# Negated rounding on ScalarE and an adding transfer for four weight tiles of the last feed-forward, with the rearrangement moved from the scaled inputs to their high and low parts

## Chip, cores and metric

The kernel runs on one core of one Trainium2 chip. The metric is the time of one execution in device microseconds, the median of several runs; less is better. Before the change it was 848.21 us (three runs, 847.84 to 849.12).

## The reference, cut to what matters

One decoder layer on 512 tokens of 1024 channels, all in float32: a half-step SwiGLU feed-forward, a mixer (a gated recurrence beside sliding-window attention), and a second half-step feed-forward, each between two RMS norms. The change touches the weights and the inputs of the feed-forwards.

```python
def swiglu(x, w_gu, w_down):
    gate, up = jnp.split(x @ w_gu, 2, axis=-1)
    return (jax.nn.silu(gate) * up) @ w_down

x = x + 0.5 * rms_norm(swiglu(rms_norm(x, ffn1_pre_g[l]), ffn1_w_gu[l], ffn1_w_down[l]), ffn1_post_g[l])
...
x = x + 0.5 * rms_norm(swiglu(rms_norm(x, ffn2_pre_g[l]), ffn2_w_gu[l], ffn2_w_down[l]), ffn2_post_g[l])
```

`w_gu` has 2 x 2816 columns, `w_down` is 2816 x 1024.

## The kernel before, in words

**Products in three passes.** Every matrix operand is held as a high part, which is the value rounded to the matrix engine's float32r format, and a low part, which is the value minus the high part. A product is high x high, high x low and low x high, summed in PSUM. So each weight tile needs a rounding copy (ScalarE, `act.copy`, line 208) and a subtraction (`low.tensor_sub`, line 213, by default on VectorE) before TensorE can use it. TensorE runs 4580 matmuls in all.

**The weight stream.** The class `Weights` holds one list of units in the order of their use. A raw block is loaded from HBM by SyncE (line 173) into one of five buffers with the tag `raw`; a unit is one weight tile made from it: `cast` is the rounding copy, `low` the subtraction. `take` hands the next unit to TensorE and first calls `fill`, which issues the casts and lows of the units that lie 3 or 4 further on. When the last unit of a raw block has had its low part issued, the next raw block's load is issued; it goes to the buffer that has been free the longest, and so waits until the readers of that buffer's last block are done. SyncE is one queue in order: a load that waits holds up every load and store behind it. While the residual stream `xT` occupies two of the five raw buffers (up to the end of the stage below), three are left.

**The stage of the change.** In the last feed-forward the first six blocks of 128 hidden channels are done in the plain way (`Hidden.classic`): for f = 2 to 5 a product `pgb` for the gate and a product `pub` for the up half, each 24 matmuls of 512 columns. Then `classic_down` multiplies by the first six blocks of rows of `ffn2_w_down`. Its weights are the units `bd`: `add_down` makes raw block `bd00` (rows f = 0 to 3, left half of the columns) with the tiles `bd00` and `bd20`, raw block `bd40` with tile `bd40`, then `bd01` with `bd01` and `bd21`, and `bd41` (right half). A tile is 128 x 1024 numbers and feeds 24 matmuls (lines 1826, 1827 and 1828: hidden high x weight high, hidden high x weight low, hidden low x weight high). Right behind it `octo(6)` begins, a Strassen-like scheme of seven products on combined weights, whose raw blocks are `bx60`, `bx61`, `by60` and `by61` and whose first weight tiles are `bp` from `bx60` and from `bx61`.

**Beside it**, spread over the same products, VectorE prepares the combined inputs of those seven products. `Next.sums(k)` scales two channel blocks by their gain and the norm factor (`xa`, `xb`, line 635), forms four differences (lines 639 to 642), and ScalarE rounds them (lines 638 and 644); `Next.lows(k)` makes their low parts (lines 651 and 655). This is done for k = 0 to 3 in each feed-forward. The tokens of these inputs stand in a rearranged order, in pieces of 32 tokens, which the scaling writes: four `scalar_tensor_tensor` per block, each for a quarter. VectorE also transposes the residual stream (`z`, line 1836), which SyncE writes to HBM as `x_hbm` in four transfers for each block (line 1839).

**Other users of the queues.** GpSimd multiplies the up and gate halves (`usb`, line 809) and issues transfers: the plain stores of partial outputs (line 1866) and, elsewhere in the program, transfers that add a tile of 128 x 512 numbers to what stands in HBM (line 1095, `accum_op=ALU.add`).

The order on each engine is the order of the code; nothing is reordered.

Of the kernel before, what the change touches and what calls it, by code (L numbers as in the profile page):

```python
# [121 lines left out]
def tile_layer(ctx: ExitStack, tc: tile.TileContext, out: bass.AP, **ins: bass.AP):  # L122
    nc = tc.nc
    pe, dve, act, pool, sync = nc.tensor, nc.vector, nc.scalar, nc.gpsimd, nc.sync
# [12 lines left out]
    HALF = [slice(0, T // 2), slice(T // 2, T)]  # L137
# [39 lines left out]
    class Deferred:  # L177


        def tensor_sub(self, *args):  # L180
            self.args = args
# [13 lines left out]
    deferred, shared = Deferred(), Shared()  # L195

    def w_tiles(nk, c, name):
        return (wpool.tile([P, nk, c], F32R, tag="whi", name=f"whi_{name}", bufs=NWS),
# [2 lines left out]
    def add_unit(r, part, nk, c, name, low=dve):  # L201
        def two(t, like):
            return t.rearrange("p k (i d) -> p k i d", i=2) if len(like.shape) == 4 else t

        def cast(raw):
            x, (hi, lo) = part(raw), w_tiles(nk, c, name)
            for ks in shared.parts if low is shared else [slice(0, nk)]:
                act.copy(two(hi, x)[:, ks], x[:, ks])
            return hi, lo

        def take_low(raw, hi, lo):
            x = part(raw)
            low.tensor_sub(two(lo, x), x, two(hi.bitcast(F32), x))

        W.unit(r, cast, take_low)
# [169 lines left out]
    def add_down(f, n, dh):  # L385

        r = W.raw(lambda: load_raw([ins["ffn2_w_down"][0, f * P:(f + n) * P, dh * T:(dh + 1) * T]], n, T, f"bd{f}{dh}"))
        for i in range(0, n, 2):
            add_unit(r, lambda raw, i=i: raw[:, i:i + 2, :], 2, T, f"bd{f + i}{dh}")

    for g, (f0, f1) in enumerate(GROUPS2):
        if g == 0:
# [174 lines left out]
    x_tiles, xT = stream()  # L567
# [8 lines left out]
    def x_low(x, src, gain, sl):  # L576
        dve.scalar_tensor_tensor(x[1][:, sl], src, gain, x[0].bitcast(F32)[:, sl], op0=ALU.mult, op1=ALU.subtract)

    def dealt(t):

        return t.rearrange("p (i b n) -> p b i n", b=NB, n=32)

    class Next:


        def __init__(self, name, pre=None, gain=None, dealt=False):

            self.name, self.pre, self.dealt = name, pre, dealt
# [32 lines left out]
        def sums(self, k):  # L621


            n = f"{self.name}{k}"
            xa, xb, t13, t24 = (wt(f"{s}_{n}") for s in ("xa", "xb", "ta", "tb"))
            b11 = t2k(f"b11_{n}", F32R)
            highs = [t2k(f"{s}h_{n}", F32R) for s in ("b2", "t13", "t24")]
            l, r = HALF
            for x, c in ((xa, k), (xb, k + 4)):
                if self.dealt:  # L630
                    d = x.rearrange("p (b i n) -> p b i n", b=NB, n=32)
                    for i in range(4):
                        row = slice(i * P, (i + 1) * P)
                        xi, ri = (t[:, row].rearrange("p (b n) -> p b n", b=NB) for t in (xT[c], self.R))
                        dve.scalar_tensor_tensor(d[:, :, i], xi, self.gain(c), ri, op0=ALU.mult, op1=ALU.mult)
                else:
                    dve.scalar_tensor_tensor(x, xT[c], self.gain(c), self.R, op0=ALU.mult, op1=ALU.mult)
            act.copy(b11[:, l], xa[:, l])
            dve.tensor_sub(t13[:, l], xa[:, r], xa[:, l])
            dve.tensor_sub(t13[:, r], xb[:, r], xa[:, r])  # L640
            dve.tensor_sub(t24[:, l], xb[:, r], t13[:, l])
            dve.tensor_sub(t24[:, r], xb[:, l], t24[:, l])
            for h, x in zip(highs, (xb, t13, t24)):
                act.copy(h, x)
            self.made = n, xa, b11, highs, (xb, t13, t24)

        def lows(self, k):

            n, xa, b11, highs, xs = self.made
            l, r = HALF  # L650
            dve.tensor_sub(b11[:, r], xa[:, l], b11.bitcast(F32)[:, l])
# [141 lines left out]
    class Hidden:  # L793
# [68 lines left out]
        def quad(self, f, last, ahead, beside=lambda i: None):  # L862

            n = f"{self.name}{f}"
            l, r = HALF
            hs = [(t2k(f"hh{n}{j}", F32R), t2k(f"hl{n}{j}", F32R)) for j in range(2)]

            def seven(b, form, first, ahead=AHEAD):
                hi, lo = W.take(ahead)
                for j in range(2):  # L870
                    o, js = b[:, HALF[j]], slice(j * P, (j + 1) * P)
                    for k in range(4):
                        xh, xl = self.nxt.t[form, k]
                        for i, (w, x) in enumerate(((hi, xh), (hi, xl), (lo, xh))):
                            pe.matmul(o, w[:, k, js], x, start=first and i + j + k == 0, stop=k == 3 and i == 2, skip_group_check=True)  # L875

            def low_parts(x, h):
                def own(t):
                    return dealt(t)[:, 2 * h:2 * h + 2] if self.nxt.dealt else t[:, HALF[h]]

                def like(t):
                    return t.rearrange("p (b i n) -> p b i n", b=2, n=32) if self.nxt.dealt else t

                for j in range(2):
                    act.copy(own(hs[j][0]), like(x[:, HALF[j]]))
                for j in range(2):
                    hh, hl = hs[j]
                    dve.tensor_sub(own(hl), like(x[:, HALF[j]]), own(hh.bitcast(F32)))
# [24 lines left out]
            dve.tensor_add(u2, u2, D)  # L913
            dve.tensor_mul(u2, p1, u2)
            W.later(1, low_parts, u2, 0)
            beside(5)
            seven(A, "b22", False, ahead)
            act.activation(g1, A, AF.Silu)
            beside(6)
            if last:  # L920
                last_half()
                low_parts(g1, 1)
            else:
                W.later(1, last_half)
                W.later(2, low_parts, g1, 1)
            for j in range(2):
                self.hs[f + j] = hs[j]
# [170 lines left out]
        return {(0, 0): B, (1, 0): Dd, (0, 1): E_, (1, 1): A}  # L1098


    n1 = Next("a", gain=lambda c: g1[:, c:c + 1], dealt=True)
    ssx = const.tile([P, 2 * NB], F32, name="ssx")
    g1 = const.tile([P, KD], F32, name="g1")

# [236 lines left out]
    for g, (f0, f1) in enumerate(GROUPS1):  # L1341
# [18 lines left out]
        for c in range(KD):  # L1360
# [25 lines left out]
            b = pair_banks[c] if c < 2 else product(W.take(), xs, name=f"ya{g}{c}")  # L1386
# [93 lines left out]
    for j in range(4):  # L1480
        b = in_product(f"pq{j}")
# [83 lines left out]
    hl = us_  # L1565
# [5 lines left out]
    scale = HD ** -0.5  # L1571
# [242 lines left out]
            W.fill(3)  # L1814
    late = [(c, W.take(0)) for c in range(EARLY, KD)]

    n2 = Next("f2", "ffn2_pre_g", dealt=True)
    banks = boundary(res, late, ysp, None, n2, "m")


# [75 lines left out]
    for g, (f0, f1) in enumerate(GROUPS2):  # L1896
# [9 lines left out]
        hs = hid.classic(f1, banks, {2.5: turns[:2], 3: turns[2:4], 3.5: [(n2.sums, 0)], 4: [(n2.lows, 0)] + turns[4:6], 4.5: [(n2.sums, 1)], 5: [(n2.lows, 1)] + turns[6:]}, AHEAD - 1)  # L1906
# [96 lines left out]
```

## Time and profile before

| | us |
|---|---|
| median of three runs | 848.21 (847.84 to 849.12) |
| the profiled execution's own time | 847.59 |
| its span, first to last instruction | 845.8 |
| TensorE busy with matmuls | 837.5 |
| VectorE busy | 726.3 |
| ScalarE busy | 516.2 |
| GpSimd busy | 187.8 |

The profile shows one execution. The span is what its rows cover; the 1.8 us between span and own time lie around it. A matmul's row is 389 ns long for 512 columns, but matmuls overlap, and the rate is read from the distance of their starts. In the list of instructions in order of time a row holds the start, the time taken, the engine, the line, the operation, what it writes and reads, and in brackets the idle time before it with what ended it. Names are those of the tiles, with buffer numbers left out, so that `wlo_bd` stands for the low part of each of the six `bd` tiles; in the rows on normalised inputs `_f` stands for the last feed-forward.

### The profile page before, as it was taken

The numbers are of one execution on the slowest core, as the hardware profiler recorded it, in microseconds if no ns is written. First come the engines' busy times: TensorE is split into PE (matmuls) and PEld (weight loads), VectorE is DVE, ScalarE is ACT, GpSimd is POOL, SyncE is SP. The second block draws the span as 40 slices with busy tenths as digits, with TensorE's granted clock in tenths as the row PEclk, the third lists the DMA queues.
The fourth block names the chain that finished last, engine by engine and source line by source line (L and its number), as shares of the span: only waits on it lengthen the run. The fifth ranks groups of instructions, "written<-read, shape, count | busy, mean of one in ns | idle before, by whom it ended". The sixth has DMA issues, their size and how long they took to land.

```text
span 845.8 us, 12561 instructions
## 1 busy us (share of the span) xinstructions
PE 837.5 (99%) x4580; PEld 727.3 (86%) x4580; DVE 726.3 (86%) x1054; ACT 516.2 (61%) x855; POOL 187.8 (22%) x199
## 2 busy tenths in 40 slices
PE   9999999999999999999999999999999999999996
PEld 8988888988988998998788899888888888888885
DVE  4988999988979866889989589698969999898996
ACT  6646856676666655556788447335655667666562
POOL 2023000230320334434455045110200014032001
PEclk9999999999999999999999999999999999999999
DMA  7249429397594899231311130166740939769742
GB/s 251 76 135 333 157 68 325 76 246 253 141 255 166 179 273 326 69 101 50 102 49 51 50 124 28 56 141 192 259 150 18 309 95 247 252 150 256 302 138 100
DMA packets 120990, 138.50 MB, mean 164 GB/s; under 512 B 23440, under 2 KB 81120, under 8 KB 120416
## 3 DMA queue, kind: packets, MB, share of 16 engines
q1 hardware_dynamic: 108816, 110.81, 40.9%
q0 software_dynamic: 11968, 26.75, 14.4%
q8 instruction: 36, 0.59, 0.3%
q14 instruction: 26, 0.21, 0.1%
q10 hardware_dynamic: 144, 0.13, 0.0%
HBM read 100.45 MB, written 37.22 MB: 163 GB/s over the span
## 4 chain that ended last, share of the span: by engine, by line
PE 97%; DVE 1%; POOL 1%; ACT 0%; issue 0%; DVEq 0%; POOLq 0%; ACTq 0%
PE aa L948 10%; PE ab L948 10%; PE db L948 5%; PE da L948 5%; PE yaa L1326 3%; PE bb L948 3%; PE ba L948 3%; PE yda L1326 2%; PE ya L501 2%; PE ya L500 2%; PE ya L499 2%; PE a_first L1185 1%; PE aa L875 1%; PE yb L1828 1%; PE yb L1827 1%; PE yb L1826 1%
## 5 line engine op out<-in xcount | busy, mean ns | idle before, releaser
L1095 POOL DMA_DIRECT2D yp_a<-stage x42 | 36.8, 1072 | 180.8 <-ACT stage L1092 162.8
L1095 POOL DMA_DIRECT2D yp_b<-stage x28 | 24.2, 1024 | 138.1 <-ACT stage L1092 122.8
L499 PE MATMUL ya<-hha,whi_ad 128*128 128x512 f32 x62 | 24.1, 389 | 0.0
L500 PE MATMUL ya<-hla,whi_ad 128*128 128x512 f32 x62 | 24.1, 389 | 0.0
L501 PE MATMUL ya<-hha,wlo_ad 128*128 128x512 f32 x62 | 24.1, 389 | 0.0
L682 POOL TENSOR_TENSOR acca_r<-acca_r,sq_r 128x512 f32<-128x512 f32 x6 | 8.0, 1327 | 45.4 <-ACT sq_r L530 45.4
L1962 POOL TENSOR_TENSOR last<-yp,grow 128x512 f32<-128x512 f32 x3 | 3.9, 1291 | 58.4 <-DVE yp L1957 58.4
L518 PE MATMUL an<-xh_mx,whi_xl 128*128 128x256 f32 x64 | 15.8, 287 | 0.0
L1958 ACT ACTIVATE ysq<-yp 128x512 f32<-128x512 f32 (+1 forms) x9 | 5.3, 585 | 16.9 <-DVE yp L1957 16.6
L519 PE MATMUL an<-xh_mx,wlo_xl 128*128 128x256 f32 x64 | 15.5, 283 | 0.0
L809 POOL TENSOR_TENSOR usb<-usb,gsb 128x512 f32<-128x512 f32 x5 | 6.4, 1295 | 35.3 <-DVE usb L806 24.0
L499 PE MATMUL gt<-xh_mx,whi_gt 128*128 128x512 f32 x32 | 14.2, 444 | 0.0
L501 PEld LDWEIGHTS ya<-hha,wlo_ad 128*128 128x128 f32 x62 | 11.6, 188 | 2.4
L500 PEld LDWEIGHTS ya<-hla,whi_ad 128*128 128x128 f32 x62 | 11.6, 188 | 2.4
L499 PEld LDWEIGHTS ya<-hha,whi_ad 128*128 128x128 f32 x62 | 11.6, 188 | 2.4
L499 PE MATMUL pub<-xh_f,whi_bu 128*128 128x512 f32 x32 | 12.6, 395 | 0.0
L501 PE MATMUL gt<-xh_mx,wlo_gt 128*128 128x512 f32 x32 | 12.6, 394 | 0.0
L499 PE MATMUL pgb<-xh_f,whi_bg 128*128 128x512 f32 x32 | 12.6, 393 | 0.0
L499 PE MATMUL pq<-xh_mx,whi_q 128*128 128x512 f32 x32 | 12.6, 393 | 0.0
L500 PE MATMUL gt<-xl_mx,whi_gt 128*128 128x512 f32 x32 | 12.6, 392 | 0.0
L501 PE MATMUL pq<-xh_mx,wlo_q 128*128 128x512 f32 x32 | 12.5, 390 | 0.0
L501 PE MATMUL pgb<-xh_f,wlo_bg 128*128 128x512 f32 x32 | 12.5, 390 | 0.0
(1962 smaller groups left out, 3502.7 us busy)
## 6 DMA issues: line engine op xcount, KB each, us to landing
yp_a<-stage POOLq DMA_DIRECT2D x50, 256.0 KB, 8.9
yp_b<-stage POOLq DMA_DIRECT2D x36, 256.0 KB, 9.1
h_a<-za SPq DMA_DIRECT2D x16, 256.0 KB, 4.5
hxa<-h_a SPq DMA_DIRECT2D x16, 256.0 KB, 19.0
h_b<-zb SPq DMA_DIRECT2D x16, 256.0 KB, 4.0
hxb<-h_b SPq DMA_DIRECT2D x16, 256.0 KB, 7.3
xn<-in_x SPq DMA_DIRECT2D x8, 256.0 KB, 4.7
xT_hbm<-xT POOLq DMA_DIRECT2D x2, 1024.0 KB, 9.6
```

The source lines that it names most:

```text
L499: pe.matmul(ps, hi[:, k, :], xh, start=start, stop=False)
L500: pe.matmul(ps, hi[:, k, :], xl, start=False, stop=False)
L501: pe.matmul(ps, lo[:, k, :], xh, start=False, stop=stop)
L518: pe.matmul(ps[:, sl], hi[:, k, :], xh, start=k == 0, stop=False)
L519: pe.matmul(ps[:, sl], lo[:, k, :], xh, start=False, stop=False)
L875: pe.matmul(o, w[:, k, js], x, start=first and i + j + k == 0, stop=k == 3 and i == 2, skip_group_check=True)
L948: pe.matmul(b[tb], x[:, blk], w[:, k, :], start=first and q + k + j == 0, stop=q + k == 2 and j == 2, skip_group_check=True)
L1095: pool.dma_start(o, st.rearrange("p (a b) -> p a b", a=2) if len(o.shape) == 3 else st, accum_op=ALU.add)
L1185: pe.matmul(banks[j][:, HALF[0]], ws[j][part][:, k, :], n1.xs[k][xpart][:, HALF[0]], start=k == 0 and part == xpart, stop=stop and k == KD ...
L1326: pe.matmul(o, a[:, k, ms], x[:, js], start=first and i + k + m % 2 == 0, stop=k == 1 and i == 2, skip_group_check=True)
L1826: pe.matmul(ps, hh[:, blk], hi[:, k, cs], start=start, stop=False, **kw)
L1827: pe.matmul(ps, hh[:, blk], lo[:, k, cs], start=False, stop=False, **kw)
```

## The change

**The low part of four weight tiles.** A class `Added` stands in for VectorE in `add_unit`. For `bd00`, `bd20`, `bd01` and `bd21` (`f + i < 4`) the low part is no longer one VectorE subtraction: ScalarE writes the negated high part into the low tile, and GpSimd issues a transfer from the raw block (in SBUF) to the low tile (in SBUF) that adds, so that raw minus high stands there. `bd40` and `bd41` keep the subtraction.

**The order of the tokens.** The scaling in `Next.sums` now writes in the natural order, one instruction per block instead of four. The four differences work on views of that (`sides`), and the rearrangement is made when ScalarE rounds (it reads through `dealt` and writes in order) and when VectorE subtracts the high part (which reads `dealt`). This holds for both feed-forwards. In `low_parts` of `quad` only the names change, since both users had the rearranged order before.

The core of the diff:

```diff
+    class Added:
+        def tensor_sub(self, lo, x, hi):
+            act.activation(lo, hi, AF.Copy, scale=-1.0)
+            pool.dma_start(lo.bitcast(F32), x, accum_op=ALU.add)
...
         for i in range(0, n, 2):
-            add_unit(r, lambda raw, i=i: raw[:, i:i + 2, :], 2, T, f"bd{f + i}{dh}")
+            add_unit(r, lambda raw, i=i: raw[:, i:i + 2, :], 2, T, f"bd{f + i}{dh}", added if f + i < 4 else dve)
...
-    def dealt(t):
-        return t.rearrange("p (i b n) -> p b i n", b=NB, n=32)
+    def dealt(t, s=slice(0, 2)):
+        return t.rearrange("p (i b n) -> p b i n", b=NB, n=32)[:, 2 * s.start:2 * s.stop]
+    def in_turn(t):
+        return t.rearrange("p (b i n) -> p b i n", i=NB, n=32)
+    def sides(t):
+        t = t.rearrange("p (i s m) -> p s i m", s=2, m=64)
+        return t[:, 0], t[:, 1]
...
             for x, c in ((xa, k), (xb, k + 4)):
-                if self.dealt:
-                    d = x.rearrange("p (b i n) -> p b i n", b=NB, n=32)
-                    for i in range(4):
-                        row = slice(i * P, (i + 1) * P)
-                        xi, ri = (t[:, row].rearrange("p (b n) -> p b n", b=NB) for t in (xT[c], self.R))
-                        dve.scalar_tensor_tensor(d[:, :, i], xi, self.gain(c), ri, op0=ALU.mult, op1=ALU.mult)
-                else:
-                    dve.scalar_tensor_tensor(x, xT[c], self.gain(c), self.R, op0=ALU.mult, op1=ALU.mult)
-            act.copy(b11[:, l], xa[:, l])
-            dve.tensor_sub(t13[:, l], xa[:, r], xa[:, l])
...
+                dve.scalar_tensor_tensor(x, xT[c], self.gain(c), self.R, op0=ALU.mult, op1=ALU.mult)
+            (al, ar), (bl, br), (t1, t3), (t2, t4) = (sides(x) for x in (xa, xb, t13, t24))
+            act.copy(in_turn(b11[:, HALF[0]]), dealt(xa, slice(0, 1)))
+            dve.tensor_sub(t1, ar, al)
...
             for h, x in zip(highs, (xb, t13, t24)):
-                act.copy(h, x)
+                act.copy(in_turn(h), dealt(x))
...
-                dve.tensor_sub(lo, x, h.bitcast(F32))
+                dve.tensor_sub(in_turn(lo), dealt(x), in_turn(h.bitcast(F32)))
```

On VectorE, before, around the first two of the four tiles (`usb4` is the scaled up product of f = 4, `f21` the inputs of k = 1):

```order
L1836 STREAM_TRANSPOSE z5_6069<-xT1_3462 128x512
L213 TENSOR_TENSOR wlo_bd00_6076<-raw_bd00_5966,whi_bd00_6075 128x1024
L806 TENSOR_TENSOR usb4_6104<-pub4_6079,R_f2_5848 128x512
L635 SCALAR_TENSOR_TENSOR xa_f21_6107<-xT0_3461,cols_137,R_f2_5848 128x4x32 x4
L635 SCALAR_TENSOR_TENSOR xb_f21_6108<-xT1_3462,cols_137,R_f2_5848 128x4x32 x4
L639 TENSOR_TENSOR ta_f21_6109<-xa_f21_6107 128x256
L640 TENSOR_TENSOR ta_f21_6109<-xb_f21_6108,xa_f21_6107 128x256
L641 TENSOR_TENSOR tb_f21_6110<-xb_f21_6108,ta_f21_6109 128x256
L642 TENSOR_TENSOR tb_f21_6110<-xb_f21_6108,tb_f21_6110 128x256
L213 TENSOR_TENSOR wlo_bd20_6132<-raw_bd00_5966,whi_bd20_6131 128x1024
L815 TENSOR_TENSOR hlb4_6163<-usb4_6104,hhb4_6162 128x512
```

The same place of VectorE in the changed kernel (its lines are numbered some 7 higher):

```order
L1840 STREAM_TRANSPOSE z5_6039<-xT1_3438 128x512
L813 TENSOR_TENSOR usb4_6075<-pub4_6050,R_f2_5824 128x512
L643 SCALAR_TENSOR_TENSOR xa_f21_6078<-xT0_3437,cols_137,R_f2_5824 128x512
L643 SCALAR_TENSOR_TENSOR xb_f21_6079<-xT1_3438,cols_137,R_f2_5824 128x512
L646 TENSOR_TENSOR ta_f21_6080<-xa_f21_6078 128x4x64
L647 TENSOR_TENSOR ta_f21_6080<-xb_f21_6079,xa_f21_6078 128x4x64
L648 TENSOR_TENSOR tb_f21_6081<-xb_f21_6079,ta_f21_6080 128x4x64
L649 TENSOR_TENSOR tb_f21_6081<-xb_f21_6079,tb_f21_6081 128x4x64
L822 TENSOR_TENSOR hlb4_6129<-usb4_6075,hhb4_6128 128x512
```

Both `wlo` subtractions are gone from VectorE's row, and eight quarter scalings have become two whole ones.

On ScalarE, in the changed kernel, from the rounding of `bd00` to that of the fifth tile (`hhb4`, `hhb5` are the rounded hidden blocks, `gsb5` a Silu):

```order
L215 CAST whi_bd00_6045<-raw_bd00_5942 128x1024
L199 ACTIVATE wlo_bd00_6046<-whi_bd00_6045 128x1024
...
L651 CAST t24h_f21_6085<-tb_f21_6081 128x512
L215 CAST whi_bd20_6096<-raw_bd00_5942 128x1024
L199 ACTIVATE wlo_bd20_6097<-whi_bd20_6096 128x1024
L821 CAST hhb4_6128<-usb4_6075 128x512
...
L821 CAST hhb5_6188<-usb5_6185 128x512
L215 CAST whi_bd01_6196<-raw_bd01_6101 128x1024
L199 ACTIVATE wlo_bd01_6197<-whi_bd01_6196 128x1024
L215 CAST whi_bd21_6201<-raw_bd01_6101 128x1024
L199 ACTIVATE wlo_bd21_6202<-whi_bd21_6201 128x1024
L215 CAST whi_bd41_6209<-raw_bd41_6158 128x1024
```

Each of the four rounding copies now has a second instruction of the same size right behind it; the rest of ScalarE's order is as before.

On GpSimd, in the changed kernel, between the products of f = 3 and the first stores:

```order
L816 TENSOR_TENSOR usb3_5969<-usb3_5969,gsb3_5923 128x512
L200 DMA wlo_bd00_6046<-raw_bd00_5942 128x1024
L816 TENSOR_TENSOR usb4_6075<-usb4_6075,gsb4_6023 128x512
L200 DMA wlo_bd20_6097<-raw_bd00_5942 128x1024
L200 DMA wlo_bd01_6197<-raw_bd01_6101 128x1024
L200 DMA wlo_bd21_6202<-raw_bd01_6101 128x1024
L1870 DMA yp_b00_5759<-stage_6320 128x512
```

The four adding transfers are new there. SyncE's order is unchanged, but two of its loads now wait for these transfers: `raw_bd41`, which takes the buffer of `raw_bd00`, and `raw_bx61`, which takes the buffer of `raw_bd01`; before, they waited for VectorE's subtractions.

More of the change, by code (lines that the diff above doesn't have):

```diff
@@ L193, in tensor_sub @@
                 eng.tensor_sub(lo[:, ks], x[:, ks], hi[:, ks])
-    deferred, shared = Deferred(), Shared()
+    class Added:
+        def tensor_sub(self, lo, x, hi):
+            act.activation(lo, hi, AF.Copy, scale=-1.0)
+            pool.dma_start(lo.bitcast(F32), x, accum_op=ALU.add)
+    deferred, shared, added = Deferred(), Shared(), Added()
     def w_tiles(nk, c, name):
@@ L577, in x_low, with __init__ @@
         dve.scalar_tensor_tensor(x[1][:, sl], src, gain, x[0].bitcast(F32)[:, sl], op0=ALU.mult, op1=ALU.subtract)
-    def dealt(t):
-        return t.rearrange("p (i b n) -> p b i n", b=NB, n=32)
+    def dealt(t, s=slice(0, 2)):
[5 more added lines that the diff above has]
+        return t[:, 0], t[:, 1]
     class Next:
-        def __init__(self, name, pre=None, gain=None, dealt=False):
-            self.name, self.pre, self.dealt = name, pre, dealt
+        def __init__(self, name, pre=None, gain=None):
+            self.name, self.pre = name, pre
             self.gain = gain or (lambda c: col(pre, c))
@@ L627, in sums @@
             highs = [t2k(f"{s}h_{n}", F32R) for s in ("b2", "t13", "t24")]
-            l, r = HALF
             for x, c in ((xa, k), (xb, k + 4)):
-                if self.dealt:
-                    d = x.rearrange("p (b i n) -> p b i n", b=NB, n=32)
-                    for i in range(4):
-                        row = slice(i * P, (i + 1) * P)
-                        xi, ri = (t[:, row].rearrange("p (b n) -> p b n", b=NB) for t in (xT[c], self.R))
-                        dve.scalar_tensor_tensor(d[:, :, i], xi, self.gain(c), ri, op0=ALU.mult, op1=ALU.mult)
-                else:
-                    dve.scalar_tensor_tensor(x, xT[c], self.gain(c), self.R, op0=ALU.mult, op1=ALU.mult)
[L638 to L642, printed above, removed]
+                dve.scalar_tensor_tensor(x, xT[c], self.gain(c), self.R, op0=ALU.mult, op1=ALU.mult)
+            (al, ar), (bl, br), (t1, t3), (t2, t4) = (sides(x) for x in (xa, xb, t13, t24))
+            act.copy(in_turn(b11[:, HALF[0]]), dealt(xa, slice(0, 1)))
+            dve.tensor_sub(t1, ar, al)
+            dve.tensor_sub(t3, br, ar)
+            dve.tensor_sub(t2, br, t1)
+            dve.tensor_sub(t4, bl, t2)
             for h, x in zip(highs, (xb, t13, t24)):
-                act.copy(h, x)
+                act.copy(in_turn(h), dealt(x))
             self.made = n, xa, b11, highs, (xb, t13, t24)
@@ L650, in lows @@
             l, r = HALF
-            dve.tensor_sub(b11[:, r], xa[:, l], b11.bitcast(F32)[:, l])
+            dve.tensor_sub(in_turn(b11[:, r]), dealt(xa, slice(0, 1)), in_turn(b11.bitcast(F32)[:, l]))
             self.t["b11", k] = b11[:, l], b11[:, r]
@@ L878, in own @@
                 def own(t):
-                    return dealt(t)[:, 2 * h:2 * h + 2] if self.nxt.dealt else t[:, HALF[h]]
-                def like(t):
-                    return t.rearrange("p (b i n) -> p b i n", b=2, n=32) if self.nxt.dealt else t
+                    return dealt(t, slice(h, h + 1))
                 for j in range(2):
-                    act.copy(own(hs[j][0]), like(x[:, HALF[j]]))
+                    act.copy(own(hs[j][0]), in_turn(x[:, HALF[j]]))
                 for j in range(2):
                     hh, hl = hs[j]
-                    dve.tensor_sub(own(hl), like(x[:, HALF[j]]), own(hh.bitcast(F32)))
+                    dve.tensor_sub(own(hl), in_turn(x[:, HALF[j]]), own(hh.bitcast(F32)))
             def last_half():
@@ L1098, in seven_down @@
         return {(0, 0): B, (1, 0): Dd, (0, 1): E_, (1, 1): A}
-    n1 = Next("a", gain=lambda c: g1[:, c:c + 1], dealt=True)
+    n1 = Next("a", gain=lambda c: g1[:, c:c + 1])
     ssx = const.tile([P, 2 * NB], F32, name="ssx")
@@ L1815, in tile_layer @@
     late = [(c, W.take(0)) for c in range(EARLY, KD)]
-    n2 = Next("f2", "ffn2_pre_g", dealt=True)
+    n2 = Next("f2", "ffn2_pre_g")
     banks = boundary(res, late, ysp, None, n2, "m")
```

## The prediction

> **What bounds the kernel now.** I read the page's busy times first, then the shares of the chain that ended last, then the busy time by stretches.
>
> ```profile
> PE 837.5 (99%) x4580; PEld 727.3 (86%) x4580; DVE 726.3 (86%) x1054; ACT 516.2 (61%) x855; POOL 187.8 (22%) x199
> PE 97%; DVE 1%; POOL 1%; ACT 0%; issue 0%; DVEq 0%; POOLq 0%; ACTq 0%
> 0.00:42.00 42.00, 40.54 (x286) 38.38 (x287) 30.84 (x84) 27.65 (x56) 5.13 (x9) 1.00 0.51 165
> 42.00:85.00 43.00, 43.00 (x191) 35.63 (x190) 36.59 (x67) 23.47 (x38) 11.05 (x13) 1.00 0.68 234
> 550.00:592.00 42.00, 42.00 (x187) 34.79 (x186) 37.22 (x71) 18.65 (x27) 2.59 (x2) 1.00 0.64 166
> 592.00:634.00 42.00, 42.00 (x187) 34.79 (x186) 33.92 (x42) 26.01 (x36) 4.36 (x8) 1.00 0.59 207
> ```
>
> TensorE (PE) is 97% of the chain. The last four rows give a stretch, its length, the busy time of PE, PE's weight loads, VectorE, ScalarE and GpSimd, the granted clock, and the DMA share and rate. The two upper ones hold the inputs' sums for the first feed-forward, the lower two the stage of the four tiles and the start of the octo. From 42 us on PE is busy for the whole length in each of them, at full clock. A busy PE could still be a slow one, so I look at the chain in order of time for the spacing:
>
> ```profile
> 575.29 0.23 PE yb L1827
> 580.73 0.23 PE yb L1827
> 591.61 0.23 PE yb L1827
> 607.70 5.44 PE ab L948 x24
> ```
>
> The first three rows are the first matmuls that read the low parts of `bd00`, `bd20` and `bd01`: these are the deadlines. They stand 5.44 us apart for each tile of 24 matmuls, the same 5.44 us that 24 matmuls take in the octo behind. So PE runs at its own pace here and waits for nobody. VectorE, 86% busy, is busy beside it. **The change therefore has nothing to gain at this place**, only deadlines to miss: no wait of PE ends with a VectorE instruction that it removes. In the first 42 us PE lacks 1.46 us; its waits show one row:
>
> ```profile
> PE warm L1172 <- POOL ident masks.py:199: 1.4, 1, 1.4
> ```
>
> That is the start of the program, which the change doesn't touch. Shorter sums in the first feed-forward give PE nothing either.
>
> **What the change removes from VectorE and adds to ScalarE.**
>
> ```profile
> 556.66 1.13 DVE L635 SCALAR_TENSOR_TENSOR xb_f<-xT,cols,R_f 128x128 f32<-128x128 f32 x4
> 566.59 1.18 DVE L213 TENSOR_TENSOR wlo_bd<-raw_bd,whi_bd 128x1024 fp32r<-128x1024 f32 x1
> 574.66 1.23 DVE L213 TENSOR_TENSOR wlo_bd<-raw_bd,whi_bd 128x1024 fp32r<-128x1024 f32 x1 [1.64 <-ACT whi_bd L208]
> 575.81 0.68 DVE L815 TENSOR_TENSOR hlb<-usb,hhb 128x512 fp32r<-128x512 f32 x1
> 584.51 2.36 DVE L213 TENSOR_TENSOR wlo_bd<-raw_bd,whi_bd 128x1024 fp32r<-128x1024 f32 x2 [0.26 <-ACT whi_bd L208]
> L577 DVE SCALAR_TENSOR_TENSOR yll<-xc,cols,ylh x4: 750/751/752, 472.6 to 479.2; 128x512 fp32r<-128x512 f32 x4
> L639 DVE TENSOR_TENSOR ta_f<-xa_f x4: 409/413/414, 557.7 to 601.4; 128x256 f32<-128x256 f32 x4
> L888 DVE TENSOR_TENSOR hla<-u2a,hha x2: 418/421/424, 314.5 to 314.8; 128x256 fp32r<-128x256 f32 x2
> L638 ACT CAST b_f<-xa_f x4: 396/407/407, 556.8 to 600.5; 128x256 fp32r<-128x256 f32 x4
> L885 ACT CAST hha<-u2a x2: 401/401/401, 314.0 to 314.3; 128x256 fp32r<-128x256 f32 x2
> ```
>
> Rows of neighbours overlap by some 0.08 us (the row at 574.66 ends at 575.89, the next starts at 575.81). Four subtractions go, 4 x 1.15 = 4.6 us. Four quarter scalings take 1.13 us together; one whole one takes 0.75 - 0.08 = 0.67 against 1.05, so a block saves 0.38, a `sums` 0.76, eight of them 6.1 us. The new views in pieces cost nothing that I can see: the 128x256 subtraction in pieces of 32 (line 888) takes 0.42 us, the contiguous one (line 639) 0.41; the ScalarE copies (lines 885 and 638) 0.40 and 0.41. I take zero, for both engines. VectorE loses 10.7 us of work, all of it beside PE: worth nothing by itself. It does make the engine earlier, which is needed below.
>
> ScalarE's rows give the times at which the four tiles are rounded:
>
> ```profile
> 563.95 1.04 ACT L208 CAST whi_bd<-raw_bd 128x1024 fp32r<-128x1024 f32 x1
> 573.59 1.04 ACT L208 CAST whi_bd<-raw_bd 128x1024 fp32r<-128x1024 f32 x1
> 582.91 0.62 ACT L814 CAST hhb<-usb 128x512 fp32r<-128x512 f32 x1 [4.15 <-DVE usb L809]
> 583.44 2.00 ACT L208 CAST whi_bd<-raw_bd 128x1024 fp32r<-128x1024 f32 x2
> 592.51 1.05 ACT L283 CAST whi_bp__6330<-raw_bx__6296 128x1024 fp32r<-128x1024 f32 x1 [0.46 <-DMA raw_bx__6296<-in_ffn_w_gu]
> 593.47 2.05 ACT L1865 ACTIVATE stage<-yb 128x512 f32<-128x512 f32 x4
> ```
>
> The negated copy has the size of the rounding copy, so I give it the same 1.04 us. It reads what that one wrote and so starts when it has ended. A round plus a negation is 2.1 us; four negations are 4 us of ScalarE, which is idle for 4.15 us ahead of `hhb` alone.
>
> **The new transfer** is the term that decides. The trace has no addition from SBUF to SBUF of 512 KB. Its nearest rows are the additions of 256 KB into HBM (line 1095), the first and the last two of eight on end, and the plain stores of 256 KB (line 1866), each with the time from issue to landing:
>
> ```profile
> L1095 POOL DMA_DIRECT2D yp_b<-stage x1: 852/852/852, 750.6 to 750.6; - x1
> DMA to landing us min/median/max: 6.7/6.7/6.7
> ...
> L1095 POOL DMA_DIRECT2D yp_b<-stage x2: 850/1016/1183, 757.3 to 757.8; - x2
> DMA to landing us min/median/max: 11.0/11.6/12.2
> ...
> L1866 POOL DMA_DIRECT2D yp_b<-stage x8: 539/539/606, 594.3 to 608.6; - x8
> DMA to landing us min/median/max: 2.4/4.2/6.0
> ```
>
> The first, with none ahead of it, takes 6.7 us. The eight from 750.6 land from 757.3 (750.6 + 6.7) to 770.0 (757.8 + 12.2): 12.7 us for seven distances, 1.8 us for each 256 KB. So twice the bytes should take 6.7 + 1.8 = **8.5 us**, two on end 3.6 us apart. The bounds: a plain 256 KB at its fastest, 2.4 us, twice that is 4.8; and twice the lone addition, 13.4. I take 8.5, since additions are the nearer kind.
>
> Here the Trainium skill says something else. "DMA: Bandwidth & Descriptors", section "Anatomy of one DMA", fits such a GpSimd transfer as about 2.0 us plus its bytes at 436 GB/s; 512 KB would then take 3.2 us, an estimate from that page, and every tile would be some 5 us early. The plain stores' 2.4 us agree with it (it gives 2.6), the additions' 6.7 us do not, and the sum goes by these.
>
> **The deadlines, one by one.**
>
> `bd00`: rounded at 563.95, or up to 0.76 earlier by the shorter sums; 563.2 + 2.1 gives the issue at 565.3 and the landing at 573.8. Wanted at 575.29. In time.
>
> `bd20`: ScalarE rounds it behind the sums of k = 1. They come 0.76 + 1.15 + 0.76 = 2.7 us earlier (two sums, one subtraction gone), so 573.59 becomes 570.9, the issue 573.0, the landing 581.5. Wanted at 580.73: **0.8 us late**, and PE waits.
>
> `bd01`: VectorE no longer waits 1.64 us for `bd20`, but its next instruction, `hlb`, waits for ScalarE's `hhb`, now behind the negation: about 573.6 in place of 575.81, 2.2 us earlier. `hhb` of f = 5 follows at 580.7 and `bd01` is rounded at 581.2, issued at 583.4, landed at 591.9. Wanted at 591.61, moved by 0.8: in time. `bd21` lands 3.6 us later, at 595.5; its deadline is 5.44 us after `bd01`'s, 597.05. In time.
>
> **What else waits.** GpSimd's multiply `usb4` stands behind the first transfer's issue and still comes before VectorE hands it its input. SyncE's loads matter more:
>
> ```profile
> 579.88 4.16 SPq L1839 DMA_DIRECT2D x_hbm<-z  x8
> 584.14 0.46 SPq L173 DMA_DIRECT2D raw_bd<-in_ffn_w_down  x1
> 586.90 0.88 SPq L173 DMA_DIRECT2D raw_bx__6296<-in_ffn_w_gu  x2
> 595.91 1.21 DVE L287 TENSOR_TENSOR wlo_bp__6331<-raw_bx__6296,whi_bp__6330 128x1024 fp32r<-128x1024 f32 x1
> 605.15 0.42 DVE L651 TENSOR_TENSOR b_f<-xa_f,b_f 128x256 fp32r<-128x256 f32 x1
> 610.26 0.62 PE L948 MATMUL ab<-whi_bp__6330,b_f 128*128 128x512 f32 x2
> ```
>
> `raw_bd41` needs `bd20`'s transfer, 581.5, and stood behind the `x_hbm` stores until 584.14 anyway (581.9 now): no loss. `raw_bx61` needs `bd21`'s, 595.5 in place of 586.90: 8.6 us later, and `by60` queues behind it. Its rounding moves from 592.51 to 601.1, in front of four stage copies (2.05 us) and the next rounding on ScalarE. From the low part of `bp` to the last `b_f` low VectorE took 605.15 - 595.91 = 9.2 us; less 0.76, and 0.7 for a rounding behind the stage copies, that is 9.1 from 602.2, with its own 0.4: 611.7. PE reads it four matmuls after 610.26, at 611.2, moved by 0.8 to 612.0. In time by 0.3 us.
>
> **Sum:** 0.8 us of waiting once, nothing gained: 847.59 + 0.8 = 848.4 for the profiled execution, 0.6 us under the median shown, so 848.21 + 0.8 = **849.0**. All three tight deadlines turn at a landing of 7.7 to 8.2 us (580.73 - 573.0 for `bd20`, 591.61 - 583.4 for `bd01`); beyond, each further us costs one.
>
> **Rivals.** (1) *Hidden.* The destination in SBUF answers faster than HBM, the landing stays under 7.7 us, PE never waits: 848.2. For it: the plain stores' 2.4 us and the skill's formula; against: every addition of half the size took at least 6.7. Chance 0.18. (2) *Slower than before by over 0.2%*: the landing time grows with the bytes as a whole, or the loads of `bd41` and `bx60` (1.5 MB beside `bd01`'s transfer) stretch it. At 13.4 us `bd20` lands at 586.4, 5.7 us late, and the octo's path moves as much: 853.9. It counts as slower from a landing of 9.4 us, 1.7 us late, at 849.9. For it: the additions that were queued took 11 to 12.2 us; against: those had seven ahead of them. Chance 0.36. (3) *Faster*: an earlier VectorE shortens what the chain spends on VectorE, 1% of the span or some 8 us; a fifth of it would give 846.5. Against: the chain runs on PE wherever the sums and the four tiles stand. Chance 0.04. (4) That the adding transfer doesn't free VectorE because `hlb` waits for ScalarE instead is in the sum already (2.2 in place of 2.7 us).
>
> **How the numbers follow.** Forecast 0.42, the rivals 0.18, 0.36, 0.04. A measurement of this kernel can tell about 0.2%, 1.7 us, from no change: within it are the forecast and the hidden case, 0.60; slower 0.36, faster 0.04. The range goes from a hidden transfer with 0.5 us of scatter, 847.7, to a landing near 12.5 us, 853.0; it leaves out the end of rival 2 and rival 3, under 2 in 10.
>
> **What would show it.** The landing of the four adding transfers: 8.5 us, 3.6 apart for the last two. PE's first read of `bd20`'s low part at 581.5 behind a wait for that DMA. `raw_bx61` issued near 595.5, released by a transfer. The scalings as single rows of 0.75 us. Wrong would be: a landing under 7 us, a wait of PE at `bd00`, differences in pieces that take more than 0.45 us, or a time below 847.

## The result, and the profile after

| | before | after |
|---|---|---|
| median, us | 847.87 (847.12 to 849.12, 15 runs) | 849.15 (848.01 to 850.43, 15 runs) |
| the profiled execution's own time, us | 847.59 | 849.90 |
| its span, us | 845.8 | 848.2 |

The changed kernel takes 1.0014 times as long (95% interval 1.0008 to 1.0021), 1.28 us more: within 0.2%, as forecast, and still a loss that can be told from nothing. The profiled execution lies 0.75 us above its median; its matmuls already reach the stage of the change 0.84 us later than before's did (the first read of `bd00`'s low part, below, is at 575.97, and at 575.13 in before). A second profile of the same kernel, further down, doesn't show this shift, so I compare places by their distances.

The page of after, busy times, the chain's shares and the costliest group with a wait:

```profile
PE 838.4 (99%) x4580; PEld 727.4 (86%) x4580; DVE 715.8 (84%) x1002; ACT 519.0 (61%) x859; POOL 193.4 (23%) x203
PE 89%; DVE 3%; DMA 2%; ACT 2%; issue 2%; POOL 1%; SPq 1%; DVEq 0%; POOLq 0%; ACTq 0%
L1831 PE MATMUL yb<-wlo_bd,hs 128*128 128x512 f32 x32 | 12.6, 395 | 1.0 <-DMA wlo_bd<-raw_bd 1.0
```

VectorE (DVE) is down from 726.3 to 715.8 us, as the change intends, and it bought nothing. A DMA is now in the chain, and the matmuls on a low part of the `bd` tiles have waited 1.0 us for one. The two longest of TensorE's waits over the whole of after (engine, line, released by: total, times, longest; the two others listed are of 0.2 us each, and neither stands in this stage):

```profile
PE warm L1176 <- POOL ident masks.py:199: 1.4, 1, 1.4
PE yb L1831 <- DMA wlo_bd<-raw_bd: 1.0, 1, 1.0
```

The first row was there before. The second is new, and it happened once. Which of the four tiles was it? TensorE's rows in order of time at the first reads of `bd00`, `bd20` and `bd01`:

```profile
575.97 0.39 PE L1831 MATMUL yb<-wlo_bd,hs 128*128 128x512 f32 x1
...
581.18 0.39 PE L1830 MATMUL yb<-whi_bd,hs 128*128 128x512 f32 x1
581.41 0.44 PE L1831 MATMUL yb<-wlo_bd,hs 128*128 128x512 f32 x1
...
592.12 0.39 PE L1830 MATMUL yb<-whi_bd,hs 128*128 128x512 f32 x1
593.55 0.50 PE L1831 MATMUL yb<-wlo_bd,hs 128*128 128x512 f32 x1 [1.04 <-DMA wlo_bd<-raw_bd]
593.89 0.40 PE L1832 MATMUL yb<-whi_bd,hs 128*128 128x512 f32 x1
594.13 0.40 PE L1830 MATMUL yb<-whi_bd,hs 128*128 128x512 f32 x1
```

Matmuls start 0.23 us apart here. At `bd20` (581.18 to 581.41) the distance holds. At `bd01` it is 1.43 us, then 0.34: 1.20 + 0.11 = **1.3 us lost, at `bd01`**, which is the whole difference of the medians. The four adding transfers, in the order `bd00`, `bd20`, `bd01`, `bd21`, with their time from issue to landing:

```profile
L200 POOL DMA_DIRECT2D wlo_bd<-raw_bd x1: 899/899/899, 566.4 to 566.4; - x1
DMA to landing us min/median/max: 5.0/5.0/5.0
...
L200 POOL DMA_DIRECT2D wlo_bd<-raw_bd x1: 899/899/899, 574.1 to 574.1; - x1
DMA to landing us min/median/max: 7.2/7.2/7.2
...
L200 POOL DMA_DIRECT2D wlo_bd<-raw_bd x1: 843/843/843, 584.4 to 584.4; - x1
DMA to landing us min/median/max: 9.1/9.1/9.1
...
L200 POOL DMA_DIRECT2D wlo_bd<-raw_bd x1: 850/850/850, 586.5 to 586.5; - x1
DMA to landing us min/median/max: 9.6/9.6/9.6
```

The same 512 KB, from SBUF to SBUF, took between 5.0 and 9.6 us. What moves beside them is in SyncE's queue, in order of time (start, duration of the issues, what is moved):

```profile
566.13 6.89 SPq L1843 DMA_DIRECT2D x_hbm<-z  x8
573.12 0.44 SPq L173 DMA_DIRECT2D raw_bd<-in_ffn_w_down  x1
578.43 4.48 SPq L1843 DMA_DIRECT2D x_hbm<-z  x8
583.07 0.39 SPq L173 DMA_DIRECT2D raw_bd<-in_ffn_w_down  x1
583.56 0.93 SPq L173 DMA_DIRECT2D raw_bx__6206<-in_ffn_w_gu  x2
596.19 0.88 SPq L173 DMA_DIRECT2D raw_bx__6258<-in_ffn_w_gu  x2
```

`bd00`'s transfer has only the `x_hbm` stores beside it; `bd20`'s starts 1 us behind the load of raw block `bd01` (1 MB, 573.12); those of `bd01` and `bd21` start right behind the loads of `bd41` and `bx60` (1.5 MB, 583.07 to 584.5).

### The profile page after: what moved, and what is told of

Read it like the earlier page. It is cut to its first block, busy times and chain, and to the rows that moved or that the text cites. A ratio compares the mean times of both kernels' runs of the same rounds, so it can differ in the third digit from the quotient of the medians.

```text
span 848.2 us, 12524 instructions
## 1 busy us (share of the span) xinstructions
PE 838.4 (99%) x4580; PEld 727.4 (86%) x4580; DVE 715.8 (84%) x1002; ACT 519.0 (61%) x859; POOL 193.4 (23%) x203
## 4 chain that ended last, share of the span: by engine, by line
PE 89%; DVE 3%; DMA 2%; ACT 2%; issue 2%; POOL 1%; SPq 1%; DVEq 0%; POOLq 0%; ACTq 0%
PE aa L952 10%; PE ab L952 10%; PE db L952 5%; PE da L952 5%; PE yaa L1330 3%; PE ba L952 3%; PE bb L952 3%; PE yda L1330 2%; PE ya L507 2%; PE ya L506 2%; PE ya L508 2%; PE a_first L1189 1%; PE aa L882 1%; PE wo L1785 1%; DMA wlo_bd<-raw_bd 1%
## 5 line engine op out<-in xcount | busy, mean ns | idle before, releaser
L1831 PE MATMUL yb<-wlo_bd,hs 128*128 128x512 f32 x32 | 12.6, 395 | 1.0 <-DMA wlo_bd<-raw_bd 1.0
L537 ACT ACTIVATE sq_r<-yp_a 128x256 f32<-128x256 f32 (+1 forms) x10 | 5.0, 502 | 12.4 <-DVE yp_a L679 5.3
L1832 PE MATMUL yb<-whi_bd,hs 128*128 128x512 f32 x32 | 12.5, 390 | 0.0
```

The costliest lines, as they stand in the source:

```text
L1831: pe.matmul(ps, hh[:, blk], lo[:, k, cs], start=False, stop=False, **kw)
L1832: pe.matmul(ps, hl_[:, blk], hi[:, k, cs], start=False, stop=stop, **kw)
```

## The experiments

**Theory T:** the whole loss is one wait of TensorE, for `bd01`'s adding transfer, and that transfer is late because other traffic, the loads of `bd41` and `bx60` above all, runs beside it. The rivals: **R**, the rearrangement (single scalings, views in pieces, sums at other times) costs something of its own; **S**, the landing time is a matter of the size or of the transfers' distance, not of what else moves. After these a third one came up, **Q**: there is a remainder of some 0.4 us beside the wait.

### The rearrangement alone

```diff
-            add_unit(..., f"bd{f + i}{dh}", added if f + i < 4 else dve)
+            add_unit(..., f"bd{f + i}{dh}", dve)
```

> Only the moved rearrangement; all six low parts are VectorE subtractions again. Theory T (the whole loss is one wait of TensorE for the adding transfer of bd01, 1.0 to 1.3 us): within 0.3 us of the kernel before, no wait in the stage of the four tiles. Theory R (the loss comes from the rearrangement, in the first feed-forward or in slower views in pieces): 1 us or more slower. VectorE should be busy some 6 us less than before.

Measured: 847.89 us (847.41 to 848.57, 11 runs) against 847.91 for before on the same chip, ratio 1.0000 (0.9991 to 1.0009), and no wait of TensorE in the stage. VectorE is busy 5.4 us less than in before (726.3 to 720.9). The interval ends below the changed kernel's 1.0014, so R falls.

### The adding transfers alone

The kernel before, with the class `Added` and its use, and the scalings in quarters as they were.

```diff
-            add_unit(..., f"bd{f + i}{dh}")
+            add_unit(..., f"bd{f + i}{dh}", added if f + i < 4 else dve)
```

> Only the four adding transfers, with the rearrangement as before. Theory T: the sums take 0.8 to 1.1 us longer each, so bd20's transfer is issued 1 to 1.5 us later than in the changed kernel, where it landed just in time; TensorE waits about 1 us at bd20 and again at bd01, together 2 to 3 us slower than before. Theory R: within 0.3 us of before.

Measured: 851.13 us (850.27 to 853.54, 5 runs), ratio 1.0041 (1.0029 to 1.0054). TensorE's waits in the stage, and where they are:

```profile
PE yb L1834 <- DMA wlo_bd<-raw_bd: 2.0, 2, 1.1
```

```profile
581.68 0.50 PE L1834 MATMUL yb<-wlo_bd,hs 128*128 128x512 f32 x1 [0.87 <-DMA wlo_bd<-raw_bd]
593.99 0.50 PE L1834 MATMUL yb<-wlo_bd,hs 128*128 128x512 f32 x1 [1.11 <-DMA wlo_bd<-raw_bd]
```

Without the shorter sums the transfer of `bd20` starts at 574.96 and lands at 581.64, and its wait appears beside that of `bd01`. So the two halves of the change belong together: the rearrangement, worth nothing alone, pays for `bd20`'s deadline. The two waits, 2.0 us by the list and 2.5 us by the distances of the matmuls' starts (1.13 + 1.38), cover the 2.4 us by which this execution (850.27) lies above before (847.91); the other four runs reach up to 853.54, and what they add I did not follow up.

### The two tiles of the right half left with VectorE

```diff
+            ... added if f + i < 4 and not dh else dve)
```

> The changed kernel with the transfer for bd00 and bd20 alone; bd01 and bd21 are VectorE subtractions again. Theory T: no wait at bd01, within 0.4 us of the kernel before (bd20's margin was only some 0.2 us). Theory R: 1.3 us slower, as the changed kernel.

Measured: 848.26 us (847.81 to 849.91, 11 runs), ratio 1.0006 (0.9997 to 1.0015), no wait of TensorE in the stage, landings of 5.0 and 7.1 us. Without the transfers of `bd01` and `bd21` the wait is gone; the interval is too wide to tell 1.0006 from 1.

### `bd01` rounded ahead of the last hidden block

In `Hidden.classic`, ahead of the last `pub` product:

```diff
+                if f == n - 1 and ahead < AHEAD:
+                    W.fill(1 + AHEAD)
                 pu = product(W.take(ahead), ...)
```

On ScalarE the rounding and the negation of `bd01` now stand ahead of `hhb5`, and its transfer is issued some 3 us sooner, before the loads of `bd41` and `bx60`.

> The changed kernel with bd01's rounding and negation ahead of the rounding of hidden block 5 on ScalarE; nothing else moves. Theory T: its transfer is issued some 3 us sooner, ahead of the loads of bd41 and bx60, lands in 5 to 8 us and before its deadline; TensorE waits for nothing here and the time is within 0.4 us of the kernel before. Theory R, or a transfer whose landing is long wherever it stands (theory S, the size alone): R 1.3 us slower; S, with a landing of 9 us, 590.5 against a deadline of 592.4, no wait either, but the landing itself tells S from T.

Measured: 848.16 us (847.79 to 849.03, 11 runs), ratio 1.0007 (0.9998 to 1.0016). The transfers of `bd01` and `bd21`:

```profile
L200 POOL DMA_DIRECT2D wlo_bd<-raw_bd x1: 843/843/843, 580.7 to 580.7; - x1
DMA to landing us min/median/max: 5.2/5.2/5.2
...
L200 POOL DMA_DIRECT2D wlo_bd<-raw_bd x1: 850/850/850, 583.4 to 583.4; - x1
DMA to landing us min/median/max: 8.6/8.6/8.6
```

The very transfer that took 9.1 us lands in 5.2 when it starts 1.8 us ahead of the loads (issued at 582.50 and 583.83 in this run); `bd21`'s, behind the first of them, takes 8.6. The size is the same, so S falls as far as size goes, and no wait of TensorE is listed. The distances of the matmuls' starts show more than that list: 0.40 us are lost at `bd20` in this run (0.29 + 0.11), where the transfer landed after 7.6 us. So that deadline has no slack either, and the expectation that TensorE waits for nothing here missed by that much.

### A load put beside `bd00`

The reverse test: the transfer that landed fastest gets 1.5 MB of company, from HBM to HBM, on ScalarE's queue. The added copy is read by nobody; it is issued at 564.69, and `bd00`'s transfer at 566.04.

```diff
+    beside = hbm.tile([3 * P, D], F32, name="beside")
...
             pool.dma_start(lo.bitcast(F32), x, accum_op=ALU.add)
+            if not self.n:
+                act.dma_start(beside, ins["ffn2_w_down"][0, :3 * P])
+            self.n += 1
```

> The changed kernel with one thing added: right ahead of the first adding transfer (bd00's, which landed after 5.04 us with little beside it) ScalarE's queue issues a copy of 1.5 MB from HBM to HBM, the weight rows of three blocks to a tile nobody reads. Theory T (what else moves at the time decides the landing): bd00's landing goes from 5.0 to between 7 and 10 us, as bd01's and bd21's with the loads of bd41 and bx60 beside them; it is wanted 9 us after its issue, so PE may wait there by at most 1 us, and the wait of about 1 us at bd01 stays as it was. Theory S (the size alone, or the distance to other additions): bd00 stays at 5.0 to 5.2 us. Only this landing is read from the run, not its time.

Measured (one profile): the first and the third transfer,

```profile
L202 POOL DMA_DIRECT2D wlo_bd<-raw_bd x1: 899/899/899, 566.0 to 566.0; - x1
DMA to landing us min/median/max: 10.7/10.7/10.7
...
L202 POOL DMA_DIRECT2D wlo_bd<-raw_bd x1: 843/843/843, 587.7 to 587.7; - x1
DMA to landing us min/median/max: 9.3/9.3/9.3
```

and TensorE's waits in the stage:

```profile
PE yb L1836 <- DMA wlo_bd<-raw_bd: 4.7, 2, 3.6
```

`bd00` goes from 5.0 to **10.7 us**, twice as long and past the 7 to 10 that T gave; the other additions are where they were, so company alone does it, and S is out. The second part of my expectation missed: the wait at `bd01` didn't stay at 1 us but grew to 3.6. The cause is one step earlier in SyncE's queue: the issues of the `x_hbm` stores took

```profile
565.76 12.77 SPq L1848 DMA_DIRECT2D x_hbm<-z  x8
578.63 1.64 SPq L173 DMA_DIRECT2D raw_bd<-in_ffn_w_down  x1
```

12.77 us in place of 6.89, the load of raw block `bd01` behind them left at 578.63 in place of 573.12, and ScalarE rounded the tile at 585.30 in place of 581.98, after it had waited 3.60 us for that load. The same company that stretched the transfer stretched the issues on SyncE's queue, and every load behind them left later.

A long wait also cost more than its own length here. Behind the one of 3.6 us the granted clock of TensorE was 0.52 from 598.0 to 601.5 us (0.98 in the microsecond before, 1.00 behind), its matmuls stood 0.43 us apart in place of 0.23, and another 1.6 us were lost. Behind the waits of about 1 us in the other runs nothing of the kind shows; whether the wait brought it on is not tested. The two waits (1.3 and 3.9 us by the distances) and this make up 6.8 of the 7.3 us by which this execution (854.92) lies above before on its chip (847.64).

### A plain transfer for `bd00`

This version leaves out the addition for one tile (its low part is then the raw value).

```diff
-            pool.dma_start(lo.bitcast(F32), x, accum_op=ALU.add)
+            pool.dma_start(lo.bitcast(F32), x, **({"accum_op": ALU.add} if self.n else {}))
+            self.n += 1
```

> The changed kernel with bd00's transfer made a plain copy of the same 512 KB from SBUF to SBUF, without the addition; the low part of that tile is then the raw value, so one product of the layer is left wrong in value and unchanged in work. It gives the price of adding by itself. If adding is what makes the 5.0 us, the plain copy lands in 2.5 to 3.7 us (the plain stores of 256 KB took 2.4 us at the fastest; the page fit of the Trainium skill, Anatomy of one DMA, gives 3.2 us); if the bytes from SBUF to SBUF make it, it stays near 5.0. The other three transfers land as in the changed kernel, 7.2, 9.1 and 9.6 us, all within 0.6, with PE's wait of 0.7 to 1.2 us at bd01.

Measured (one profile), `bd00`'s plain transfer and `bd20`'s adding one:

```profile
L200 POOL DMA_DIRECT2D wlo_bd<-raw_bd x1: 583/583/583, 565.9 to 565.9; - x1
DMA to landing us min/median/max: 3.5/3.5/3.5
...
L200 POOL DMA_DIRECT2D wlo_bd<-raw_bd x1: 914/914/914, 573.6 to 573.6; - x1
DMA to landing us min/median/max: 5.6/5.6/5.6
```

Plain 3.5 us, adding 5.0: the addition costs 1.5 us of 512 KB. The formula of the Trainium skill ("DMA: Bandwidth & Descriptors", "Anatomy of one DMA"), 3.2 us by its figures, comes within 0.3 us of the plain transfer, and near none of the adding ones. The transfers of `bd01` and `bd21` landed in 8.9 and 9.4 us, with a wait of TensorE of 1.0 us at `bd01`, as expected. `bd20` was expected within 0.6 us of 7.2 and landed in 5.6: in this run the load of `bd01`'s block was issued 2.2 us ahead of it (571.47), in after 1.0 us (573.12), so less of it ran beside. The other runs with whole transfers and no load put beside lie on the same scale: 7.6 us when the load stood 0.8 us ahead (`bd01` sooner), 6.7 to 7.1 when it stood 1.6 us ahead (three runs). That fits T, and warns that these landings move by 2 us with small shifts of the neighbours.

### Each transfer in two halves

```diff
-            pool.dma_start(lo.bitcast(F32), x, accum_op=ALU.add)
+            for k in range(2):
+                pool.dma_start(lo.bitcast(F32)[:, k], x[:, k], accum_op=ALU.add)
```

> The changed kernel with each of the four adding transfers issued as two of 256 KB, so that the matmuls on the first half of a tile wait for the first half alone and the second half is wanted 12 matmuls, 2.7 us, later. Theory T (the whole loss is the one wait for bd01's transfer, which came 1 us late): the first half lands sooner than the whole did (3.5 to 4.5 us with nothing beside it, 6 to 8.5 us for bd01), the second half issued 0.9 us later lands at about the old time but is wanted 2.7 us later, so the wait goes or falls under 0.3 us and the time comes to 847.9 to 848.5, ratio 1.000 to 1.0007 against 1.0014 for the changed kernel. If two transfers of 256 KB cost more together than one of 512 KB, as 1.8 us for each further addition into HBM would make it, the wait stays near 1 us and the time near 849.1.

Measured: 848.06 us (847.41 to 848.94, 11 runs) against 847.64 for before on this chip, ratio 1.0005 (0.9996 to 1.0014). The first half of `bd00`, and the two halves of `bd01`:

```profile
L201 POOL DMA_DIRECT2D wlo_bd<-raw_bd x1: 902/902/902, 565.9 to 565.9; - x1
DMA to landing us min/median/max: 3.8/3.8/3.8
...
L201 POOL DMA_DIRECT2D wlo_bd<-raw_bd x2: 846/1008/1170, 584.3 to 584.8; - x2
DMA to landing us min/median/max: 7.4/7.8/8.1
```

256 KB land in 3.8 us, the whole 512 KB in 5.0 (both with the `x_hbm` stores beside), so some 1.2 us for the further 256 KB. Beside the loads the first half of `bd01` still takes 7.4 us in place of 9.1, the second is wanted 2.7 us later, and TensorE lists no wait in the stage; by the distances 0.20 us are lost at `bd01`. T's number, and a remedy that costs four more instructions on GpSimd.

### Both remedies, the changed kernel and the rearrangement again, on one chip

The three versions without a wait stood at 1.0005 to 1.0007, which left Q open. So the two remedies together (`bd01` sooner, transfers in halves), the changed kernel and the rearrangement alone ran side by side.

> The changed kernel with both remedies: bd01 rounded and its addition issued ahead of the last hidden block, and each addition in two of 256 KB. Theory T (one wait of TensorE is the whole loss): no wait for these transfers is left, excess distances of the matmuls' starts 0 to 0.2 us between 560 and 600, and the time is that of the rearrangement alone, ratio to before 0.9998 to 1.0003. A remainder theory, Q: the three versions without a wait measured so far stood at 1.0005 to 1.0007, so the additions or the negations may cost 0.4 us in some other way (busier queues, the delayed loads); then this version stands at 1.0004 to 1.0008 as well. Nothing in it can be faster than before, since TensorE does the same work.

> The changed kernel itself once more, beside the other two on one chip. Theory T and Q both: 1.0 to 1.4 us over before, ratio 1.0011 to 1.0017, with a wait of TensorE for bd01's addition of 0.8 to 1.2 us. By T the distance to the version with both remedies is that whole difference, by Q only 0.7 to 1.0 us of it.

> The rearrangement alone (all low parts by VectorE) once more, beside the other two. Both theories: ratio 0.9995 to 1.0005. It is the zero against which T and Q are read: by T the version with both remedies stands within 0.2 us of it, by Q 0.3 to 0.6 us above it.

| | us | ratio to before (847.80, 27 runs) |
|---|---|---|
| both remedies | 847.77 (847.26 to 848.47, 11 runs) | 0.9999 (0.9990 to 1.0008) |
| the changed kernel | 849.07 (847.95 to 850.18, 11 runs) | 1.0016 (1.0007 to 1.0024) |
| the rearrangement alone | 847.95 (847.68 to 848.46, 11 runs) | 1.0002 (0.9993 to 1.0011) |

The changed kernel's TensorE shows the same wait a second time:

```profile
PE yb L1831 <- DMA wlo_bd<-raw_bd: 1.1, 1, 1.1
```

With both remedies there is none, neither in the list nor by the distances, with all four negations and additions still in the kernel, and the 1.3 us are gone whole (849.07 to 847.77). T stands. The interval reaches up to 1.0008, so a small remainder isn't excluded, but nothing is left for Q to explain; and part of what raised it, 1.0005 and 1.0007, has a place: the 0.20 and 0.40 us lost by the distances in the versions with halves and with `bd01` sooner. No version beat the kernel before: TensorE's matmuls are the same, and in this stage before loses nothing between them.

## Why the prediction was right, and where it wasn't

The sign and nearly the size were right (+0.8 us forecast, +1.28 measured), and so was the mechanism, a change that can only miss deadlines. The place was wrong.

- **TensorE is the bound, VectorE's relief is worth nothing: right.** VectorE lost 10.5 us (10.7 forecast) and the rearrangement alone changed the time by 0.02 us.
- **Prices on VectorE and ScalarE: right**, with one exception. The negation takes 1.06 us (1.04), the differences in pieces 0.41, and the single scaling:

```profile
L643 DVE SCALAR_TENSOR_TENSOR xa_f<-xT,cols,R_f 128x512 f32<-128x512 f32 x4 | 3.0, 740 | 0.0
L643 DVE SCALAR_TENSOR_TENSOR xb_f<-xT,cols,R_f 128x512 f32<-128x512 f32 x4 | 5.1, 1267 | 0.0
```

  0.74 us, but 1.27 on average for `xb_f`; two of its four took 1.78 and 1.79 us (last section). The saving came out all the same, since before lost as much there: its two scalings of `xa_f` and `xb_f` took 2.19 + 1.13 us in four quarters each, where after's took 0.74 + 1.78, 0.8 us less (0.76 forecast).
- **When the transfers are issued: right.** With the 0.84 us of this execution added, the forecast gives 573.8 for `bd20` and 584.2 for `bd01`; they were issued at 574.11 and 584.42.
- **How long they take: this step failed.** The prediction took "8.5 us", one number for all four, from additions into HBM. Measured were 5.0, 7.2, 9.1 and 9.6. Two errors nearly cancelled, and that 849.0 came so close to 849.15 is luck. An addition into SBUF lands far sooner than one into HBM: 3.8 us for 256 KB where the row used had 6.7; the rival *Hidden* had that part right. And what runs beside it stretches it up to twofold: 9.1 against 5.2 for the same tile behind and ahead of the loads. That the loads of `bd41` and `bx60` could stretch it stood in rival 2 and not in the sum. "Beyond, each further us costs one" is not safe either: with the load beside `bd00`, a wait of 3.6 us was followed by another 1.6 us at a lower clock.
- **Hence the deadlines came out crossed.** "0.8 us late" for `bd20`: it landed at 581.31 (574.11 + 7.2), and TensorE read it at 581.41 without a gap. "In time" for `bd01`: it landed at 593.51, due at 592.35 (592.12 + 0.23). Even 8.5 us would have been 0.6 us too long there (584.42 + 8.5 = 592.92): the prediction had it in time only because it let the wait at `bd20` move the deadline. Its deadlines are also 0.16 us late, since rows of the chain start behind the matmuls' own starts (575.13, 580.57 and 591.45 in before), and of the "three" that turn at 7.7 to 8.2 us it works out two.
- **SyncE's later loads: right in time, too pessimistic behind.** `raw_bx61` was issued at 596.19 (595.5 + 0.84 = 596.3 forecast). The octo's path, "in time by 0.3 us", was not tight: ScalarE, which waited for that load, began to round it at 600.00, 3.8 us after its issue, not at 601.1 + 0.8. VectorE's last `b_f` low part and the first matmul on `bx61`'s weights:

```profile
610.18 0.42 DVE L658 TENSOR_TENSOR b_f<-xa_f,b_f 128x256 fp32r<-128x256 f32 x1
```

```profile
612.54 0.62 PE L952 MATMUL ab<-whi_bp__6292,b_f 128*128 128x512 f32 x2
```

  The low part is there at 610.6 and wanted four matmuls after 612.54, at 613.4: 2.8 us to spare.

## What to carry to other kernels

On a kernel whose bound engine never waits, moving work off another engine is a list of new deadlines; write each with the slack it has and the traffic that shares its time. A transfer that stands in for an engine's instruction has no price of its own: take its lone time and its time beside the heaviest neighbour, and check the deadline against the second. If one misses by a microsecond, issue it ahead of the large loads or in pieces that are waited for one by one, and nothing may have to be given up, as here. A long miss may cost more than its own length, as one run suggests.

## What the runs showed of the hardware

- **Adding in flight has a price.** 512 KB from SBUF to SBUF: 3.5 us plain (one run), 5.0 to 5.1 us adding (`bd00` in five runs). The Trainium skill ("Collectives: The Full Stack", "The bandwidth ceiling: the fold count and why AG ≠ RS ≠ AR") says of a reduce step that its add needs two reads for each write and halves the rate. With twice the bytes in the formula above that would make 4.4 us, an estimate from the two pages; the measured step of 1.5 us is of that kind (1.2 by the estimate). The pages speak of transfers between cores and of plain ones; no run here looks at the reads themselves.
- **The issues of stores stretch beside such transfers.** The issues of eight `x_hbm` stores took 4.79 us in before (4.12 with the rearrangement alone), 5.69 beside the plain transfer, 6.89 in after, 12.77 with the 1.5 MB beside. SyncE's next load waits that long.
- **A scaling can be held by GpSimd, whole or in quarters.** The two scalings of 1.78 and 1.79 us are those that start while GpSimd multiplies. VectorE's and GpSimd's rows in after:

```profile
567.20 0.73 DVE L643 SCALAR_TENSOR_TENSOR xa_f<-xT,cols,R_f 128x512 f32<-128x512 f32 x1
567.85 1.79 DVE L643 SCALAR_TENSOR_TENSOR xb_f<-xT,cols,R_f 128x512 f32<-128x512 f32 x1
```

```profile
567.43 1.66 POOL L816 TENSOR_TENSOR usb<-usb,gsb 128x512 f32<-128x512 f32 x1
```

  `xa_f`, which began before the multiply (567.43 to 569.09), took its 0.73 us; `xb_f`, which began during it, ended 0.55 us behind it. The Trainium skill ("SBUF — State Buffer", "SBUF: two separate sides") describes a port pair that VectorE and GpSimd share as an exclusive lock for a whole instruction; these rows agree within 0.2 us. In before one of four quarters took 1.41 us beside the multiply, where the others took 0.34, so about the same microsecond was lost there:

```profile
554.54 2.19 DVE L635 SCALAR_TENSOR_TENSOR xa_f<-xT,cols,R_f 128x128 f32<-128x128 f32 x4
```

  VectorE had the time to lose, before and after.
